# Two buffers instead of three for the low half of a split weight, and a twelfth buffer for raw weights

## The chip, the cores and the metric

The kernel runs on one core of one Trainium2 chip. The metric is the device time of one launch in microseconds (us). Before the change the median of three runs was 1666.89 us (1665.35 to 1670.17).

## The reference

A two-layer encoder trunk over 256 tokens of width 1024, all in float32. Every layer is a mixer, a memory cross-attention and a feed-forward part, each added to the residual stream:

```
for l in range(2):
    xn = rmsnorm(x, norm_mix[l])
    x = x + (even_mixer if l == 0 else odd_mixer)(xn, ...)
    x = x + memory_cross_attention(rmsnorm(x, norm_mem_q[l]), rmsnorm(mem, norm_mem_kv[l]), w_q, w_kv, w_o)
    h = rmsnorm(x, norm_ffn[l])
    x = x + (swiglu(h, gate, up, down)           # width 2816, layer 0
             if l == 0 else moe_swiglu(h, ...))  # top 2 of 8 experts of width 3584, layer 1
return rmsnorm(x, norm_final)
```

The even mixer is a gated MLP over blocks of 128 tokens beside a forgetting attention, whose logits get the cumulated log of a forget gate as a bias. The odd mixer is a differential attention with a relative bias beside a short gated convolution. The weights are read once: 95 MB before the experts and 336 MB in the eight experts.

## The kernel before

**Pieces.** All weights come in pieces of 1 MB (128 partitions x 2048 floats). `load_w` (L108) does three things with each. SyncE's queue (SP) issues the DMA into a raw buffer (L106). ScalarE (ACT) copies the raw piece into `wh`, rounded to the engine format fp32r, in two instructions of 128x1024 (L121). VectorE (DVE) writes the rest, raw minus `wh`, into `wl` (L123), in two instructions of 128x1024 before the experts and in one of 128x2048 in them. TensorE (PE) then multiplies three times: `wh` by the high and by the low half of the activations (L138 and L141, alternating), and after these `wl` by the high half (L144). In three of the eight experts, the small ones (places 2, 4 and 7, at most 64 tokens each), two products are made (L996), again the one with `wl` last. So `wl` is read in the last third or half of a piece's work on PE.

**Buffers.** `wh` and `wl` come from one pool (`wsplit`, L63) with three buffers each. The subtraction for piece j can start when the raw piece has landed, its `wh` is written, and PE has read the `wl` of piece j-3 for the last time. The raw buffers are two before the experts (`rawp`). For the experts the room of tiles that are not needed any more is taken as well, and a pool `raw2` of `RAW2` = 3 buffers is opened: eleven in all, used in turn. The DMA into a raw buffer waits until the subtraction of the piece that had it before has ended.

**Order.** The program is written in one order and a scheduler gives each engine a fixed list at build time, by its own model of what becomes ready when. An engine works through its list in order: an instruction that waits holds up all that stand behind it. In `issue_after` regions (`behind`) the kernel ties an instruction to another by hand. So the place of a split instruction among the norm, softmax and routing steps of its engine depends on when the scheduler believed that a buffer would be free.

**Names.** `cb` (L491, L492) is the bias of the forgetting attention: `cvec` (the cumulated gates) is written to DRAM and read back on all partitions by a DMA from GpSimd's queue (L473), and DVE then adds the mask in two steps. `qT` and `kT` (L478, L481) are that attention's queries and keys, projected from four pieces (0 to 3); `elg` are its logits, `mh`/`ml` and `nh`/`nl` the split memory tokens and the split normalised activations, `tps` transposes on PE, `xs` (L163, L282) and `ms` (L149) steps of a norm. `gcr`/`gcp` (L213, L215) fetch and transpose the gain of the router's norm. `ge` (L906) is the exponential in the router's gates, `sg` (L1032) the SiLU of an expert's gate product, `sgs` (L1028) the copy that stands at that place in a small expert.

**Experts.** An expert has 42 pieces in four chunks of its width: gate, the down projection of the chunk before, up. 128 (or 64) gathered tokens stand still and the weights move. The end (`finish`, L1179 on) scatters the last expert's output and norms the result. The gain of the final norm lies in the buffer that the rotation gives at that point.

Of the kernel before, what the change touches and what calls it, by code (L numbers as in the profile page):

```python
# [12 lines left out]
F32R = mybir.dt.float32r  # L13
# [7 lines left out]
P = 128  # L21
# [6 lines left out]
DFF = 2816  # L28
DFFE = 3584
NE = 8  # L30
RAW2 = 3
WSPLIT = ((0, 0, 4), (1, 0, 4), (0, 4, 8), (1, 4, 8))
WSPLIT_MOE = ((0, 0, 4), (0, 4, 8), (1, 0, 8))
CHUNKS = ((0, 1024), (1024, 1024), (2048, 1024), (3072, 512))
# [21 lines left out]
def trunk_kernel(ctx: ExitStack, tc: tile.TileContext, io, out, stop=None):  # L56
# [37 lines left out]
    def pick(kind):  # L94
        lst = pools[kind]
        p = lst[cnt[kind] % len(lst)]
        cnt[kind] += 1
        return p

    def load_raw(src, a, b, parts=1):  # L100
        p, tag = pick("raw")
        r = p.tile([P, a, b], F32, tag=tag, name="raw")
        m = a // parts
        for i in range(parts):
            with behind(*gate):
                chain["dma"] = nc.sync.dma_start(r[:, i * m:(i + 1) * m, :], src[:, i * m:(i + 1) * m, :])  # L106
            gate.clear()
        return r  # L108

    def load_w(src, a, b, parts=1):  # L110
        r = load_raw(src, a, b, parts)
        p = pick("w")
        wh = p.tile([P, a, b], F32R, tag="wh", name="wh")
        wl = p.tile([P, a, b], F32R, tag="wl", name="wl")
        rf, hf, lf = (v.rearrange("p a b -> p (a b)") for v in (r, wh, wl))
        n = a * b // parts
        for part in range(parts):
            for i, c0, c1 in pools["split"]:
                sl = slice(part * n + c0 * n // 8, part * n + c1 * n // 8)
                if i == 0:  # L120
                    chain["wh"] = nc.scalar.activation(hf[:, sl], rf[:, sl], AF.Copy)  # L121
                elif i == 1:
                    chain["wl"] = nc.vector.tensor_sub(lf[:, sl], rf[:, sl], hf[:, sl].bitcast(F32))  # L123
                else:
                    nc.gpsimd.tensor_sub(lf[:, sl], rf[:, sl], hf[:, sl].bitcast(F32))
        return wh, wl

    def split_to(hi, lo, src):
        return (nc.scalar.activation(hi, src, AF.Copy),  # L129
                nc.vector.tensor_sub(lo, src, hi.bitcast(F32)))  # L130
# [107 lines left out]
    pA = ctx.enter_context(tc.tile_pool(name="acts", bufs=1))  # L238
    ps2 = ctx.enter_context(tc.tile_pool(name="xs", bufs=2))
    with ExitStack() as pre:  # L240
# [48 lines left out]
        def proj_ws(act, w, ncols, c0, into=None):  # L289

            ah, al = act
            wh, wl = load_w(w[:, c0:c0 + 256].rearrange("(k p) n -> p k n", p=P), KT, 256)
            ps = mmp.tile([P, 2, S], F32, tag="mm", name="pws") if into is None else into
            for f in range(2):
                o = ps[:, f, :]
                mm3([(o, wh[:, k, f * P:(f + 1) * P], wl[:, k, f * P:(f + 1) * P], ah[:, k, :], al[:, k, :])
                     for k in range(KT)], True, True, True)
            return ps
# [476 lines left out]
    with ExitStack() as moe:  # L775
        mA = moe.enter_context(tc.tile_pool(name="macts", bufs=1))
        sm = moe.enter_context(tc.tile_pool(name="msmall", bufs=2))
        m2 = moe.enter_context(tc.tile_pool(name="macts2", bufs=2))
        raw2 = moe.enter_context(tc.tile_pool(name="raw2", bufs=RAW2))

        def mbank(shape, name="mm"):
            return trp.tile(shape, F32, tag="tr", name=name)
# [294 lines left out]
        def split_y(yacc, n, pool=mA, tag="y"):  # L1077
            y = pool.tile([P, 2, 512], F32R, tag=tag, name="y")
            split_to(y[:, 0, :], y[:, 1, :], yacc[n])
            return y  # L1080

        def scatter(e, st, y, n):
            sl = slice(n * 512, (n + 1) * 512)
            for t in range(2):
                ps = mbank([P, 512], "sc")
                for i in range(2):
                    nc.tensor.matmul(ps, st[:, t, :], y[:, i, :], start=i == 0, stop=i == 1)
                nc.vector.scalar_tensor_tensor(x[t][:, sl], ps, comb[:, t, e:e + 1], x[t][:, sl],  # L1088
                                               op0=OP.mult, op1=OP.add)
# [4 lines left out]
        if done(4):  # L1094
            return
        pools["raw"] = ([(rawp, "raw")] + [(pA, tag) for tag in ("mh", "ml", "nh", "nl", "K")]
                        + [(raw2, "raw")] * RAW2 + [(pA, "V"), (rawp, "raw")])
        cnt["raw"] = cnt["w"] = 0
# [34 lines left out]
        for e in range(NE):  # L1133
            for c in range(nch):
# [32 lines left out]
                if prev is not None:  # L1167
                    pe, pc, phT, nacc = prev
# [7 lines left out]
                if c == 0:  # L1176
                    yacc = [mmp.tile([P, 512], F32, tag="mm", name=f"y{n}") for n in range(2)]
# [24 lines left out]
        pe, pc, hT, yacc = prev  # L1202
# [3 lines left out]
            down(pc, hT, yacc, i, w2[i])  # L1206

        def last_scatter(n):
            scatter(pe, st, split_y(yacc, n, pA, ("gain", "nh")[n]), n)
        finish(gf, last_scatter)  # L1210


        cv = nc.values_load(cint[0:1, NE:NE + 1], min_val=0, max_val=S + CAP - SCAP,
                            skip_runtime_bounds_check_because="a count of 256 tokens lies in 0..256")
        with tc.If(cv > CAP):
            for e in range(NE):
                for r0 in range(SCAP if e in SMALL else CAP, S, P):
# [26 lines left out]
                    st = m2.tile([P, 2, P], F32, tag="st", name="st_o", bufs=1)  # L1244
# [66 lines left out]
```

## Time and profile before

| | |
|---|---|
| median of three runs | 1666.89 us |
| the profiled execution | 1662.44 us |
| its span in the trace | 1660.7 us |
| PE busy | 1565.1 us (94%) |
| DVE busy | 1263.7 us (76%) |
| ACT busy | 1074.4 us (65%) |
| granted TensorE clock, mean | 0.993 |

The span is what the trace covers, from the first to the last instruction; 1.7 us of the execution lie around it. The busy share is a mean over stages. Until about 640 us (mixers, attentions, dense feed-forward) PE is nearly always busy and DVE is idle for more than a third of the time; in the experts, from about 640 to 1645 us, DVE is busy for 81 to 91% of each stretch, and the DMA engines for 74 to 99%. A row of the timeline gives the start, the duration (of all, where several are taken together: x2, x4), the engine, the line, the operation and its tiles, and in brackets how long the engine stood idle before it and what ended the wait.

### The profile page before, as it was taken

What the parts mean: (1) busy time and instruction counts of PE and PEld (TensorE: products, weight loads), DVE (VectorE), ACT (ScalarE), POOL (GpSimd) and SP (SyncE); (2) the same over time, 40 slices, a digit from 0 to 9 for tenths busy, and PEclk for the clock granted to TensorE, in tenths of its full rate; (3) what the DMA queues carried; (4) which work ended last, traced back from release to release, by engine and by line L of the source; (5) the groups of instructions that cost most, each with busy time, mean ns of one, the idle gap of its engine ahead of it and who ended that gap; (6) DMA issues with size and microseconds to landing.
All of it is one profiled execution on the core that took longest, in us unless ns stands there. A gap on an engine that the chain in (4) does not pass through costs nothing. (4 is left out here: it accounts for less than half of the span.)

```text
span 1660.7 us, 22384 instructions
## 1 busy us (share of the span) xinstructions
PE 1565.1 (94%) x8432; PEld 1305.1 (79%) x8432; DVE 1263.7 (76%) x1216; ACT 1074.4 (65%) x1396; POOL 46.9 (3%) x75
## 2 busy tenths in 40 slices
PE   8999999999999999999999889999888999999885
PEld 7889889999989887888887667777667777777653
DVE  5785665445576657899988888978988978888875
ACT  5555553444554446787777787677777766777775
POOL 1010010000000102000000000000000000000000
PEclk9999999999999999999999999999999999999998
DMA  7556465565535586999999999999999999999980
GB/s 248 166 185 207 145 224 195 180 201 178 190 128 178 185 333 245 345 346 348 359 361 364 350 351 349 339 334 386 341 356 349 333 346 344 339 338 347 356 304 28
DMA packets 175585, 465.03 MB, mean 280 GB/s; under 512 B 9118, under 2 KB 64438, under 8 KB 175340
## 3 DMA queue, kind: packets, MB, share of 16 engines
q1 hardware_dynamic: 174412, 459.80, 77.2%
q0 software_dynamic: 1056, 3.72, 0.7%
q8 instruction: 68, 1.11, 0.3%
q14 instruction: 49, 0.40, 0.1%
HBM read 462.42 MB, written 2.11 MB: 280 GB/s over the span
## 5 line engine op out<-in xcount | busy, mean ns | idle before, releaser
L123 DVE TENSOR_TENSOR wl<-raw,wh 128x2048 fp32r<-128x2048 f32 (+1 forms) x527 | 983.5, 1894 | 232.5 <-ACT wh L121 229.2
L121 ACT ACTIVATE wh<-raw 128x1024 fp32r<-128x1024 f32 x866 | 852.6, 1049 | 280.3 <-PE pws L141 95.1
L138 PE MATMUL gu<-wh,ch 128*128 128x512 f32 x560 | 220.6, 394 | 2.8 <-ACT sg L1032 2.8
L141 PE MATMUL gu<-wh,cl 128*128 128x512 f32 x560 | 219.2, 392 | 0.1
L144 PE MATMUL gu<-wl,ch 128*128 128x512 f32 x560 | 152.8, 395 | 10.5 <-DVE wl L123 10.5
L138 PE MATMUL pws<-nh,wh 128*128 128x256 f32 x560 | 137.2, 283 | 0.0
L141 PE MATMUL pws<-nl,wh 128*128 128x256 f32 x560 | 137.2, 283 | 0.0
L144 PEld LDWEIGHTS gu<-wl,ch 128*128 128x128 f32 x560 | 103.5, 188 | 40.3 <-DVE wl L123 19.1
L138 PEld LDWEIGHTS gu<-wh,ch 128*128 128x128 f32 x560 | 105.1, 188 | 27.1 <-ACT sg L1032 2.9
L996 PE MATMUL gu<-wl,ch 128*128 128x512 f32 x336 | 99.2, 417 | 25.3 <-DVE wl L123 24.3
L141 PEld LDWEIGHTS gu<-wh,cl 128*128 128x128 f32 x560 | 105.2, 188 | 21.9 <-DVE cl L1113 0.5
L141 PE MATMUL y<-wh,hs 128*128 128x512 f32 x280 | 110.9, 396 | 0.0
L138 PE MATMUL y<-wh,hs 128*128 128x512 f32 x280 | 110.4, 394 | 0.0
L138 PEld LDWEIGHTS pws<-nh,wh 128*128 128x128 f32 x560 | 105.9, 189 | 1.3 <-ACT wh L121 0.9
L141 PEld LDWEIGHTS pws<-nl,wh 128*128 128x128 f32 x560 | 105.9, 189 | 0.4
L996 PEld LDWEIGHTS gu<-wl,ch 128*128 128x128 f32 x336 | 58.3, 189 | 56.4 <-DVE wl L123 47.5
L996 PE MATMUL gu<-wh,ch 128*128 128x512 f32 x336 | 96.7, 402 | 4.4 <-ACT wh L121 4.0
L138 PE MATMUL acc<-wh,ch 128*128 128x512 f32 x216 | 84.7, 392 | 0.0
L141 PE MATMUL acc<-wh,cl 128*128 128x512 f32 x216 | 84.4, 391 | 0.0
L996 PEld LDWEIGHTS gu<-wh,ch 128*128 128x128 f32 x336 | 62.7, 190 | 23.6 <-ACT wh L121 10.7
L144 PE MATMUL y<-wl,hs 128*128 128x512 f32 x280 | 79.1, 404 | 2.0 <-DVE wl L123 2.0
L144 PE MATMUL pws<-nh,wl 128*128 128x256 f32 x560 | 78.8, 283 | 0.0
(363 smaller groups left out, 2177.7 us busy)
## 6 DMA issues: line engine op xcount, KB each, us to landing
raw<-in_moe_w_up_dram SPq DMA_DIRECT2D x112, 1024.0 KB, 7.1
raw<-in_moe_w_gate_dram SPq DMA_DIRECT2D x112, 1024.0 KB, 6.7
raw<-in_moe_w_down_dram SPq DMA_DIRECT2D x110, 1024.0 KB, 6.6
raw<-in_mem_w_kv_dram SPq DMA_DIRECT2D x16, 1024.0 KB, 5.2
raw<-in_odd_w_in_dram SPq DMA_DIRECT2D x12, 1024.0 KB, 5.2
raw<-in_ffn_w_gate_dram SPq DMA_DIRECT2D x11, 1024.0 KB, 5.1
raw<-in_ffn_w_up_dram SPq DMA_DIRECT2D x11, 1024.0 KB, 5.1
raw<-in_ffn_w_down_dram SPq DMA_DIRECT2D x11, 1024.0 KB, 4.8
```

Source lines behind the costliest of these rows:

```text
L121: chain["wh"] = nc.scalar.activation(hf[:, sl], rf[:, sl], AF.Copy)
L123: chain["wl"] = nc.vector.tensor_sub(lf[:, sl], rf[:, sl], hf[:, sl].bitcast(F32))
L138: mm = nc.tensor.matmul(ps, ah, bh, start=f, stop=False, skip_group_check=bank)
L141: nc.tensor.matmul(ps, *((ah, bl) if w_left else (al, bh)), start=False, stop=False, skip_group_check=bank)
L144: mm = nc.tensor.matmul(ps, *((al, bh) if w_left else (ah, bl)), start=False, stop=e, skip_group_check=bank)
L996: mm = nc.tensor.matmul(ps, a, b[which], start=f, stop=e)
```

## The change

`wl` gets a buffer count of its own, two, so that the subtraction for piece j waits until PE has read the `wl` of piece j-2 (before: j-3). `wh` keeps three. The room, 8 KB in each partition, goes to a fourth buffer of `raw2`: the rotation in the experts has twelve raw buffers instead of eleven. With twelve, the buffers that the gain of the final norm and the last piece come to lie in are others, and the second half of the last scatter takes the room of `mh` instead of `nh`.

```
-RAW2 = 3
+RAW2 = 4
...
         wh = p.tile([P, a, b], F32R, tag="wh", name="wh")
-        wl = p.tile([P, a, b], F32R, tag="wl", name="wl")
+        wl = p.tile([P, a, b], F32R, tag="wl", name="wl", bufs=2)
...
-            scatter(pe, st, split_y(yacc, n, pA, ("gain", "nh")[n]), n)
+            scatter(pe, st, split_y(yacc, n, pA, ("gain", "mh")[n]), n)
```

The scheduler gives other lists to DVE, ACT, PE and SP from the start to the beginning of the third expert. GpSimd's list, and from there on those of the four engines, are the same as before.

The first place is DVE's list in the forgetting attention, where the bias `cb` is made. Each L123 of 128x1024 is half a piece. Before:

```order
L468 TENSOR_SCALAR fncs<-fcs 4x256
L123 TENSOR_TENSOR wl<-raw,wh 128x1024 x4
L491 TENSOR_TENSOR cb<-cb,cmask 128x4x128
L492 TENSOR_TENSOR cb<-cb,cmask 128x4x128
L123 TENSOR_TENSOR wl<-raw,wh 128x1024
L149 TENSOR_SCALAR ms<-ss 128x1
L282 SCALAR_TENSOR_TENSOR xs<-xs,rs,gain 128x1024
```

And now:

```order
L468 TENSOR_SCALAR fncs<-fcs 4x256
L123 TENSOR_TENSOR wl<-raw,wh 128x1024 x2
L491 TENSOR_TENSOR cb<-cb,cmask 128x4x128
L123 TENSOR_TENSOR wl<-raw,wh 128x1024 x2
L492 TENSOR_TENSOR cb<-cb,cmask 128x4x128
L123 TENSOR_TENSOR wl<-raw,wh 128x1024
L149 TENSOR_SCALAR ms<-ss 128x1
```

The four halves ahead of `cb` are pieces 2 and 3. Piece 3, the second one of the keys, now stands behind the first step of `cb`.

The second place is ACT's list in the first expert, third chunk: the router's two `ge` and the two `sg` among the copies of the weights (numbers in the names tell the pieces apart). Before:

```order
L121 ACTIVATE wh_6749<-raw_6747 128x1024
L906 ACT_TABLE_LOAD
L906 ACTIVATE ge_6512<-ge_6512,comb_5835 128x1
L121 ACTIVATE wh_6749<-raw_6747 128x1024
L121 ACTIVATE wh_6768<-raw_6766 128x1024
L906 ACTIVATE ge_6532<-ge_6532,comb_5835 128x1
...
L121 ACTIVATE wh_6817<-raw_6815 128x1024 x2
L1032 ACT_TABLE_LOAD
L1032 ACTIVATE sg_6822<-gu_6640,rs_6272 128x512
L1032 ACTIVATE sg_6822<-gu_6641,rs_6272 128x512
```

And now:

```order
L906 ACT_TABLE_LOAD
L906 ACTIVATE ge_6512<-ge_6512,comb_5835 128x1
...
L1032 ACT_TABLE_LOAD
L1032 ACTIVATE sg_6822<-gu_6640,rs_6272 128x512
L906 ACT_TABLE_LOAD
L906 ACTIVATE ge_6532<-ge_6532,comb_5835 128x1
...
L1032 ACT_TABLE_LOAD
L1032 ACTIVATE sg_6822<-gu_6641,rs_6272 128x512
```

The first `sg` has moved in between the two `ge`, and with it ACT loads its function table four times where it loaded it twice.

The third place is ACT's list where the third expert, the first of the small ones, begins. Before:

```order
L121 ACTIVATE wh_8118<-raw_8116 128x1024 x2
L121 ACTIVATE wh_8135<-raw_8133 128x1024 x2
L1028 ACTIVATE sgs_8207<-gu_8069,rs_7941 128x512
L1028 ACTIVATE sgs_8207<-gu_8070,rs_7941 128x512
L121 ACTIVATE wh_8150<-raw_8148 128x1024 x2
```

And now:

```order
L121 ACTIVATE wh_8118<-raw_8116 128x1024 x2
L121 ACTIVATE wh_8135<-raw_8133 128x1024 x2
L121 ACTIVATE wh_8150<-raw_8148 128x1024 x2
L1028 ACTIVATE sgs_8207<-gu_8069,rs_7941 128x512
L1028 ACTIVATE sgs_8207<-gu_8070,rs_7941 128x512
```

The copy of one piece (`wh_8150`) has moved ahead of the two `sgs`.

## Rows read from the trace of the kernel before

**Rows 1.** The page: engines' busy time, DMA share in 40 slices, issue to landing
```profile
PE 1565.1 (94%) x8432; PEld 1305.1 (79%) x8432; DVE 1263.7 (76%) x1216; ACT 1074.4 (65%) x1396; POOL 46.9 (3%) x75
...
raw<-in_moe_w_up_dram SPq DMA_DIRECT2D x112, 1024.0 KB, 7.1
```
**Rows 2.** Windows: us, busy PE, PEld, DVE, ACT, POOL; clock, DMA share, GB/s
```profile
640.00:760.00 120.00, 117.15 (x549) 97.01 (x548) 109.36 (x125) 96.11 (x110) 1.95 (x2) 1.00 0.91 339
760.00:883.00 123.00, 123.00 (x555) 100.96 (x555) 110.64 (x68) 94.84 (x104) 0.00 (x0) 1.00 0.99 365
```
**Rows 3.** Waits, SP's queue, 640 to 1645 us: total us, times, longest
```profile
SPq L106 <- DVE wl L123: 618.8, 264, 6.7
```
**Rows 4.** Waits of DVE for landing pieces, 600 to 1645 us (all)
```profile
DVE wl L123 <- DMA raw<-in_moe_w_up_dram: 2.2, 3, 1.0
DVE wl L123 <- DMA raw<-in_moe_w_gate_dram: 0.8, 2, 0.5
```
**Rows 5.** Timeline, DVE: one piece of the dense feed-forward, one of the second expert
```profile
304.30 2.36 DVE L123 TENSOR_TENSOR wl<-raw,wh 128x1024 fp32r<-128x1024 f32 x2 [3.34 <-ACT wh L121]
...
808.62 2.29 DVE L123 TENSOR_TENSOR wl<-raw,wh 128x2048 fp32r<-128x2048 f32 x1 [0.47 <-ACT wh L121]
```
**Rows 6.** Timeline, PE: products with `wl`, two pieces earlier and same piece
```profile
308.72 1.12 PE L144 MATMUL pwu<-nh,wl 128*128 128x256 f32 x8
...
317.08 1.12 PE L144 MATMUL pws<-nh,wl 128*128 128x256 f32 x8
...
809.05 1.08 PE L144 MATMUL gu<-wl,ch 128*128 128x512 f32 x4
...
814.64 1.09 PE L144 MATMUL y<-wl,hs 128*128 128x512 f32 x4
```
**Rows 7.** Timeline, DVE, around `cb`
```profile
26.90 2.36 DVE L123 TENSOR_TENSOR wl<-raw,wh 128x1024 fp32r<-128x1024 f32 x2 [0.55 <-ACT wh L121]
36.72 0.69 DVE L491 TENSOR_TENSOR cb<-cb,cmask 128x512 f32<-128x512 f32 x1 [7.46 <-DMA cb<-cvec]
37.33 0.69 DVE L492 TENSOR_TENSOR cb<-cb,cmask 128x512 f32<-128x512 f32 x1
```
**Rows 8.** Timeline, PE, around piece 3 and the logits
```profile
35.82 1.11 PE L144 MATMUL pws<-nh,wl 128*128 128x256 f32 x8
...
41.26 1.09 PE L265 MATMUL tps<-ident,xs 128*128 128x128 f32 x8 [1.26 <-DVE ms L149]
...
46.21 1.22 PE L499 MATMUL elg<-kT,qT 128*128 128x256 f32 x2 [0.55 <-DVE ml L130]
```
**Rows 9.** Timeline, ACT and SP: copies of pieces 4 and 5, issues
```profile
36.70 2.94 ACT L121 ACTIVATE wh<-raw 128x1024 fp32r<-128x1024 f32 x3
...
26.38 3.28 SPq L106 DMA_DIRECT2D raw<-in_even_w_in_dram  x2
```
**Rows 10.** Timeline, PE: waits in the odd layer
```profile
423.82 0.63 PE L265 MATMUL tps<-ident,xs 128*128 128x128 f32 x4 [0.70 <-DVE xs L163]
...
485.79 0.30 PE L714 MATMUL ont<-ident,on 128*128 128x128 f32 x1 [0.87 <-DVE on L710]
...
550.60 0.19 PE L215 MATMUL gcp<-ident,gcr 8*128 8x8 f32 x1 [2.48 <-DMA gcr<-in_norm_ffn_dram]
```
**Rows 11.** Timeline, ACT: table loads in the first expert
```profile
706.46 1.28 ACT L906 ACT_TABLE_LOAD   x1
707.76 0.29 ACT L906 ACTIVATE ge<-ge,comb 128x1 f32<-128x1 f32 x1
...
718.96 1.28 ACT L1032 ACT_TABLE_LOAD   x1
```
**Rows 12.** Timeline, DVE and PE: the piece that follows the table loads
```profile
718.92 2.28 DVE L123 TENSOR_TENSOR wl<-raw,wh 128x2048 fp32r<-128x2048 f32 x1
...
721.84 1.09 PE L144 MATMUL y<-wl,hs 128*128 128x512 f32 x4
```
**Rows 13.** Timeline, DVE: entry of the third expert
```profile
890.42 8.89 DVE L123 TENSOR_TENSOR wl<-raw,wh 128x2048 fp32r<-128x2048 f32 x4 [2.06 <-ACT wh L121]
```

## Prediction
> **What bounds the kernel now.** I read the page first: PE is busy for 1565.1 us of a span of 1660.7 us, at nearly the full granted clock [rows 1]. What PE does isn't changed, so the time can move only by PE's idle stretches, some 96 us in all. Then the windows: in the first expert PE is busy for 117.15 of 120 us and in the second for all of 123, while DVE has 109.36 and 110.64 us of work [rows 2]. So in these two experts, and in everything before them, PE is the bound, and DVE runs ahead of it. Third, the waits. SP's queue waits 618.8 us, 264 times, for a subtraction to release a raw buffer [rows 3]: the engines that eat the weights pace the DMA, not the other way round. In all the experts DVE waits 3.0 us, five times, for a piece to land [rows 4], and ACT and PE never. Last the timeline at the places where the new lists differ from the old.
>
> **The twelfth raw buffer: 0.** A piece lands some 7.1 us after its issue [rows 1]. A deeper queue can at most remove the 3.0 us of [rows 4]; it doesn't move the pace. Bounds 0 and -3.0; I take 0, since only the release changes, and that comes from the same subtractions.
>
> **The missing third `wl` buffer where nothing is moved: 0.** In the dense feed-forward, DVE subtracts a piece at 304.30 [rows 5], and PE first uses it at 317.08; the piece two earlier is read until 308.72 + 1.12 = 309.84 [rows 6]. With two buffers the subtraction starts there, 5.5 us later, and ends at 309.84 + 2.36 = 312.2: 4.9 us early still. In the second expert the subtraction at 808.62 [rows 5] would wait for 809.05 + 1.08 = 810.13, end at 812.42, and be needed at 814.64 [rows 6]: a lead of 3.7 us shrinks to 2.2. The other pieces of both stages repeat this with a lead that stays above 1.7 us. What is queued behind a waiting subtraction on DVE (a split of activations, an `sg`) comes up to 1.5 us later and has about that much to spare. Price 0, if the cover is gone up to 1.5 us per place.
>
> From the third expert on the lists are the same, and DVE isn't three pieces ahead of PE any more: the third buffer lies unused, and the rest of the run is moved as a whole.
>
> **What the new lists cost.** Four places carry the sum.
>
> *The bias `cb`: +3.5 us.* Its first step waits on a DMA and starts at 36.72, after 7.46 us of idleness. Piece 3 was subtracted before that, from 26.90 to 29.26 [rows 7], and PE wanted it at 35.82 [rows 8]. Now it stands behind that step: it can run from 37.33 and takes 2.36 us, to 39.69. Of PE's eight products the first four could run once the first half is there, at 38.5; the other four, due at 35.82 + 0.48 = 36.30, wait for 39.69: PE is 3.4 us late. Part of it falls into idle time that PE has right behind: 1.26 us at 41.26 for the memory norm and 0.55 us at 46.21 for the logits [rows 8]. The norm on DVE, though, stands behind `cb`'s second step, which ends at 39.69 + 0.6 instead of 38.0, so these waits move along by 2.3 us. That is the lower end. The upper end comes from SP: the raw buffer of piece 3 goes to piece 5, whose DMA was the second of two that SP had issued by 29.66 [rows 9], right after the subtraction. Now it is issued at 39.7. It lands between 42.6 (1 MB at the 365 GB/s of [rows 2]) and 46.8 (the 7.1 us of [rows 1]). ACT has piece 5's two copies (the last two of the three at 36.70 [rows 9], 2.0 us) ahead of the second `kT` and the memory's `mh` (0.6 us each), and DVE's `ml` needs 0.6 more. With the early landing this is done before the norm's transposes; with the late one the first `ml` is there at 50.6, and the logits, before at 46.21, come 4.5 us late. Value 3.5, about the middle of 2.3 to 4.5.
>
> *Norms and softmaxes before the experts: +3.1 us.* Halves of a subtraction that wait for PE now stand ahead of steps that PE waits for. In the norm before the odd mixer a half (1.2 us) comes between the residual and `xs`; PE's wait of 0.70 us there [rows 10] grows by up to as much: +0.7. In the differential attention two halves move in between the softmax steps (+1.2) and a piece of 2.36 us moves out from ahead of the norm for which PE waits 0.87 us [rows 10]: +0.5. At the router's gain PE arrives four products of 0.235 us earlier at a transpose that waits for a DMA of its own, 2.48 us now [rows 10]: +0.9. A few like these (the first softmax, the memory attentions, the routing) are worth 0 to 2 together, and I take 1.0. Sum 3.1, range 0 to 4.1: a wait that PE meets late anyway, after the 3.5 us, can swallow a part.
>
> *The table loads: +1.0 us.* The first expert's third chunk has two more of them, 1.28 us each [rows 11]: 2.56 us more on ACT, and one `sg` of 0.65 us earlier in the list, all ahead of the copy that releases the subtraction at 718.92. That copy was done 1.9 us before it. So the subtraction starts 1.3 us later and ends at 722.5; PE wants it at 721.84 [rows 12], 0.65 us late, and the second `sg` with its table load makes it about 1.0 in the next piece but one. Range 0 to 2.6, the whole of the ACT time.
> The Trainium skill ("ScalarE: Activation LUTs", What ACT_TABLE_LOAD costs) gives a switch 1283 ns for the load and some 1380 ns for a drain, 2.66 us together. Here the load ends at 707.74 and the next activation starts at 707.76 [rows 11]: the load agrees, the drain doesn't show. By the page the two loads would be 5.3 us, and this term some 2.7 us larger, near 3.7; I go by the row.
>
> *The third expert's entry: -1.2 us.* DVE waits 2.06 us for a copy at 890.42 [rows 13]; ACT now has it ahead of two `sgs` of 1.27 us together. DVE sets the pace there, so about that much is gained, less a little for `sgs`. Range -2.1 to 0.
>
> **The sum.** 3.5 + 3.1 + 1.0 - 1.2 = +6.4 us. The profiled execution took 1662.44 us (span 1660.7), so it would take 1668.8. It lies 4.45 us below the median of the runs shown, which is within their spread; the same +6.4 on the median gives 1673.3 us.
>
> **Rivals.**
> *No change.* The 3.4 us at piece 3 are swallowed by later waits for DMAs that come at a fixed time, and the small terms are lost in PE's idle time. Before the third expert PE idles some 18 us in all, so there is room. Against it: the largest of these waits are themselves behind the chain that is delayed. +0 to +3, about 1668.
>
> *Faster.* It has its place at the entry of the third expert: the copy moved ahead there gives all 2.06 us [rows 13], the twelfth buffer removes the 3.0 us of waits for landing pieces [rows 4], and `cb` costs only what doesn't fit into the 1.81 us of PE's idle time right behind it, 1.6. Together -3.5 us, with the 3.1 of the norms hidden: 1663.4. It decides when the bias lands: if `cvec` comes 3 us earlier, piece 3 costs nothing, and it is -5. Against it: nothing in the change makes that DMA earlier.
>
> *A bubble in each piece.* The Trainium skill ("Perfetto Trace Analysis", Identifying Performance Opportunities) says that the same gap again and again on the busiest engine can mean too few buffers for the next tile. As a mechanism here: each of the 83 pieces from the fourth of the first expert to the end of the second starts its subtraction only when PE has finished the piece two before, DVE loses up to 1.5 us of its lead each time, and its spare time (12.4 of 123 us in the second expert, 10.6 of 120 in the first [rows 2]) is used up. If a fifth of the 83 come 0.5 us late, that is 8 us more: 1681.7. Against it: the loss of a lead is paid once and not per piece, as PE's use and DVE's start are then tied at a distance of two pieces.
>
> That the change doesn't do what it says isn't likely: the lists differ, and the buffer counts are fixed at build time.
>
> **How the numbers follow.** About 0.3% (5 us) is what a measurement of this kernel tells from no change. Forecast (+2 to +12) 0.62, no change (0 to +3) 0.22, bubbles (+12 to +18) 0.07, faster (-5 to 0) 0.09. Of the forecast's case two thirds lie above +5, the rest counts as the same: slower 0.42 + 0.07 + 0.04 for runs that a small shift in the medians takes over the bound = 0.53; faster 0.07, since of the faster case only a part passes the bound, and the base of three runs is itself uncertain; same 0.40. The range takes in the terms' bounds: their lower ends give 2.3 + 0 + 0 - 2.1 - 3.0 = -2.8, their upper ends 4.5 + 4.1 + 2.6 + 0 = +11.2, and 2 us of spread of the runs on the upper side: 1664 to 1680.5.
>
> **What would show it.** Right: in the new trace PE waits 3 us for `wl` at about 36 to 40 us; the logits start at 49 to 51; the wait before `gcp` is near 3.4; ACT has four table loads between 705 and 730; DVE's 2.06 us at the third expert are gone; and from there to the end both traces run at one distance, 6.4 us. Wrong: if PE has new waits for `wl` all through the first two experts, it is the bubbles; if the distance is under 2 us at 640 us, the order cost nothing; if it changes between the third expert and the end, the claim that the rest is only moved fails.

## The result, and the profile after

The changed kernel takes 1678.2 us (median of five runs, 1674.0 to 1679.84), the kernel before on the same chip 1665.68 us (1665.32 to 1670.17). The ratio is 1.0065, with a 95% interval of 1.0051 to 1.0079: 10.8 us slower (0.0065 x 1666). The profiled execution took 1674.0 us, its span is 1672.1 us.

The page of the kernel after; it answers to the first line of [rows 1]:

```profile
PE 1570.2 (94%) x8432; PEld 1305.6 (78%) x8432; DVE 1263.7 (76%) x1216; ACT 1080.4 (65%) x1398; POOL 47.8 (3%) x75
```

ACT has two instructions and 6 us more, GpSimd 0.9 us more; PE has the same 8432 products and 5.1 us more for them; its mean granted clock is 0.991, and was 0.993. PE's idle time in the span grew from 95.6 to 101.9 us.

The waits of SP's queue, 640 us to the end, as [rows 3]:

```profile
SPq L106 <- DVE wl L123: 649.1, 272, 8.1
```

The subtractions still pace the DMA. DVE's waits for landing pieces, 3.0 us in [rows 4], have no row any more.

The windows of the kernel after, first expert, with the columns of [rows 2]:

```profile
640.00:760.00 120.00, 113.65 (x517) 92.94 (x516) 101.15 (x117) 91.65 (x104) 7.09 (x4) 0.97 0.86 317
```

GpSimd works 7.09 us in this stretch, where it had 1.95: its piece came later. The granted clock was 1.00 and is 0.97.

The best view is a difference of two traces: take the time at which each piece's last product ends on PE, subtract the time of the same product in the trace of before, and see by how much this distance grows in each stretch (us; the stretches go by the times of before, and those left out move by 0.2 or less in every column). Names of the columns are those of the experiments below; *again* is the same kernel profiled once more.

| stretch of before, us | what lies there | after | again | x_pre3 | x_pool | x_gates | x_cb | x_all |
|---|---|---|---|---|---|---|---|---|
| 0 to 34 | first pieces | -0.6 | -0.5 | -0.6 | +1.8 | +0.3 | -0.2 | +0.1 |
| 34 to 72 | `cb` | -0.1 | +0.1 | +0.9 | +1.3 | +2.5 | +0.2 | -2.6 |
| 72 to 423 | layer 0 | +2.3 | +2.7 | -0.2 | +3.1 | +2.4 | +2.0 | +2.4 |
| 423 to 538 | odd norm, differential attention | +1.5 | +1.5 | +0.2 | +1.5 | +1.5 | +1.5 | +1.5 |
| 538 to 556 | router's gain | +0.8 | +0.5 | -1.6 | +0.9 | +1.0 | +0.7 | +0.8 |
| 556 to 640 | layer 1 to the experts | 0.0 | +0.1 | +2.6 | 0.0 | +1.6 | +1.1 | -0.1 |
| 640 to 651 | first pieces of the experts | **+4.0** | **+4.0** | **+4.0** | 0.0 | +4.0 | +4.0 | 0.0 |
| 657 to 672 | first SiLU | +1.4 | +2.7 | +0.5 | +1.5 | +2.8 | +2.8 | +1.5 |
| 712 to 762 | table loads | +1.8 | +1.8 | +1.8 | +1.8 | +0.4 | +1.8 | +0.4 |
| 877 to 902 | entry of the third expert | -0.7 | -0.7 | -0.7 | +1.0 | -0.7 | -0.7 | +1.0 |
| 902 to 1569 | the rest | -0.3 | +0.1 | +0.5 | +0.5 | +0.2 | +0.1 | -0.3 |
| 1569 to the end | | +1.5 | +0.3 | +0.8 | 0.0 | +1.0 | +0.3 | +1.5 |
| all | | 11.7 | 12.6 | 8.4 | 13.4 | 17.0 | 13.7 | 6.4 |

The profiled execution of before was a short one (1662.44 us), so these totals lie above what the ratios say. A term that is the same to 0.1 us in several columns belongs to the kernel; of one that changes from profile to profile (the first and the last row, `cb`, the first SiLU) a single column says little.

The largest term stands in no sentence of the prediction. GpSimd's timeline at the start of the experts, before and then after:

```profile
635.42 6.53 POOL L125 TENSOR_TENSOR wl<-raw,wh 128x512 fp32r<-128x512 f32 x4 [0.87 <-ACT wh L121]
```

```profile
644.27 7.09 POOL L125 TENSOR_TENSOR wl<-raw,wh 128x512 fp32r<-128x512 f32 x4 [5.86 <-issue]
```

GpSimd subtracts the experts' third piece (L125, in four quarters). Before, it did so as soon as `wh` was there; now it waits for PE's first piece and starts 8.85 us later, of which 3.9 are the distance that everything had by then. DVE and PE of the kernel after in the same place:

```profile
638.62 2.29 DVE L123 TENSOR_TENSOR wl<-raw,wh 128x2048 fp32r<-128x2048 f32 x1
...
646.95 3.29 DVE L123 TENSOR_TENSOR wl<-raw,wh 128x2048 fp32r<-128x2048 f32 x1 [4.24 <-issue]
```

```profile
651.41 0.50 PE L144 MATMUL gu<-wl,ch 128*128 128x512 f32 x1 [2.06 <-POOL wl L125]
```

And the tile `wl` there, count and shortest/median/longest in ns, then first and last start:

```profile
L125 POOL TENSOR_TENSOR wl<-raw,wh x4: 1300/1308/3329, 644.3 to 648.0; 128x512 fp32r<-128x512 f32 x4
L123 DVE TENSOR_TENSOR wl<-raw,wh x2: 2286/2788/3290, 638.6 to 646.9; 128x2048 fp32r<-128x2048 f32 x2
```

DVE starts the next piece at 646.95, while GpSimd is at its third quarter: DVE's subtraction takes 3.29 us instead of 2.29, GpSimd's last quarter 3.33 instead of 1.30, and PE stands idle for 2.06 us. The other 2 us are clock: in 650 to 660 us the granted clock was 0.83 (row with x_apart below).

The two engines met before the change too. GpSimd's quarters in the trace of before:

```profile
L125 POOL TENSOR_TENSOR wl<-raw,wh x4: 1287/1288/2767, 635.4 to 640.7; 128x512 fp32r<-128x512 f32 x4
```

The first quarter took 2.77 us, beside DVE's subtraction of 634.75 to 637.03. PE didn't need the piece yet, and no wait of PE came of it.

### The profile page after: what moved, and what is told of

Same layout as the page of the kernel before. It is cut to its first block, busy times and chain, and to the rows that moved or that the text cites. A ratio compares the mean times of both kernels' runs of the same rounds, so it can differ in the third digit from the quotient of the medians.

```text
span 1672.1 us, 22491 instructions
## 1 busy us (share of the span) xinstructions
PE 1570.2 (94%) x8432; PEld 1305.6 (78%) x8432; DVE 1263.7 (76%) x1216; ACT 1080.4 (65%) x1398; POOL 47.8 (3%) x75
## 5 line engine op out<-in xcount | busy, mean ns | idle before, releaser
L123 DVE TENSOR_TENSOR wl<-raw,wh 128x2048 fp32r<-128x2048 f32 (+1 forms) x527 | 986.1, 1897 | 230.6 <-ACT wh L121 85.0
L144 PE MATMUL gu<-wl,ch 128*128 128x512 f32 x560 | 154.5, 397 | 12.6 <-DVE wl L123 10.5
```

Of the source, the lines that this page charges most:

```text
L144: mm = nc.tensor.matmul(ps, *((al, bh) if w_left else (ah, bl)), start=False, stop=e, skip_group_check=bank)
```

## The experiments

One run is the changed kernel once more; all others are edits of it or of the kernel before that alter order or buffers, and all compute the whole reference. Ratios are to the kernel before, run beside each.

**x_wl2: two `wl`, eleven raw buffers.** The half of the change without the twelfth raw buffer; the lines are those in which it differs from the changed kernel.

```
-RAW2 = 4
+RAW2 = 3
...
-            scatter(pe, st, split_y(yacc, n, pA, ("gain", "mh")[n]), n)
+            scatter(pe, st, split_y(yacc, n, pA, ("gain", "nh")[n]), n)
```

> One part alone: two wl buffers, eleven raw buffers. Theory 1 (the whole loss comes from the lists and waits that the missing wl buffer makes): the lists are those of the changed kernel up to the last expert, so 1676 to 1680 us, ratio to before near 1.0065, and the distance to the trace of before follows that of the changed kernel piece by piece. Rival (the twelfth raw buffer, and the places it gives to the gain of the final norm, cost something): back by a few us, 1668 to 1674, with the distance different in the last expert.

Measured: 1681.21 us, ratio 1.0096 (1.0075 to 1.0117). All of the losses are there (+4.0 and +1.8 among them), and the entry of the third expert costs +0.97 where the changed kernel has -0.69: the lists are those of after but for this place, where `wh_8150` stands behind the `sgs` again, and the end. DVE at the entry:

```profile
907.60 6.70 DVE L123 TENSOR_TENSOR wl<-raw,wh 128x2048 fp32r<-128x2048 f32 x3 [1.89 <-ACT wh L121]
```

So the losses are owed to `wl`, and the gain at the entry to the twelfth raw buffer; whether through the list or through the buffer itself, x_wl2sgs asks.

**x_pool: GpSimd's piece gets a raw buffer for its `wl`,** so that it need not wait for PE.

```
-        wl = p.tile([P, a, b], F32R, tag="wl", name="wl", bufs=2)
+        wl = spare.tile([P, a, b], F32R, tag="raw", name="wl") if spare else p.tile([P, a, b], F32R, tag="wl", name="wl", bufs=2)
...
-            w_first.append(gate_piece(wg, 0, 0, 2))
+            w_first.append(gate_piece(wg, 0, 0, 2, raw2))
```

> The changed kernel, but the wl of the experts' third piece, the one that GpSimd subtracts, gets a room of its own (one of the raw2 buffers), so it need not wait for PE to read the first piece. Theory 1 (GpSimd's 7 us start 9 us later because of that wait, PE idles 2.1 us and its clock falls for some us after it): GpSimd's start goes back from 644 to about 639, PE's idle 2.06 us at 651 are gone, the distance at the experts' fourth piece is 3.9 and not 7.9 us, and if the second stretch of low clock (670 to 680 us) follows from the first, another 1.3 us are gone: 1672 to 1674 us. Rival (what is lost there is the lists' order on DVE, where pieces wait for PE): the distance still grows to 7 to 8 us by the fourth piece and the time stays at 1677 to 1680.

Measured: 1675.26 us, 1.0054 (1.0035 to 1.0074). GpSimd:

```profile
643.88 6.56 POOL L125 TENSOR_TENSOR wl<-raw,wh 128x512 fp32r<-128x512 f32 x4 [0.83 <-ACT wh L121]
```

It starts 8.46 us later than in before, which is just the distance of this run at that point (8.5), and the first pieces of the experts cost 0.05 instead of 4.0. The ratio isn't clearly below that of the changed kernel (1.0065, and 1.0051 when it ran again): ACT's list at the third expert falls back to that of before and takes 1.7 us of the 4.0 back (+1.0 there instead of -0.7). The 1672 to 1674 us that were expected were missed. GpSimd and DVE overlap here as well:

```profile
L125 POOL TENSOR_TENSOR wl<-raw,wh x4: 1279/1292/2806, 643.9 to 649.1; 128x512 fp32r<-128x512 f32 x4
```

One quarter takes 2.81 us, and PE doesn't wait: an overlap that comes early enough costs nothing.

**x_gates: the first `sg` of the third chunk stays behind the second `ge`,** as before.

```
-                nc.scalar.activation(ge[:, 1:2], ge[:, 0:1], AF.Exp, scale=comb[:, t, NE:NE + 1])
+                chain["ge"] = nc.scalar.activation(ge[:, 1:2], ge[:, 0:1], AF.Exp, scale=comb[:, t, NE:NE + 1])
...
-                sg = gated(e, gu, rs)
+                with behind(*(("ge",) if (e, c) == (0, 2) else ())): sg = gated(e, gu, rs)
```

> The changed kernel, with the first expert's third sg tied behind the second ge of the router, so that ACT loads its table twice there and not four times. Theory 1 (the two more loads of 1.28 us cost the 1.8 us by which the distance grows at 727 to 740 us): PE's wait of 1.32 us at 733 is gone, the distance stays at 9.2 us there, time 1675 to 1677. Rival (two wl buffers cost it, since DVE's lead is thin there anyway): the distance grows to 11 as before, time unchanged.

Measured: 1677.42 us, 1.0070 (1.0047 to 1.0093): no gain that the ratio could show, but the term falls from 1.8 to 0.4. The first expert's third chunk in the kernel after, ACT and then PE, and PE in x_gates:

```profile
716.67 1.28 ACT L906 ACT_TABLE_LOAD   x1
...
720.44 1.28 ACT L1032 ACT_TABLE_LOAD   x1
...
722.44 1.28 ACT L906 ACT_TABLE_LOAD   x1
...
731.64 1.28 ACT L1032 ACT_TABLE_LOAD   x1
```

```profile
732.78 1.20 PE L144 MATMUL y<-wl,hs 128*128 128x512 f32 x4 [1.32 <-DVE wl L123]
```

```profile
738.21 1.20 PE L144 MATMUL y<-wl,hs 128*128 128x512 f32 x4 [0.26 <-DVE wl L123]
```

With two loads instead of four PE's wait for that `wl` shrinks from 1.32 to 0.26 us.

**x_cb: both steps of `cb` stay behind piece 3,** as before.

```
-            nc.vector.tensor_tensor(cb[:, :, S:384], ...
+            with behind("wl"): nc.vector.tensor_tensor(cb[:, :, S:384], ...
-            nc.vector.tensor_tensor(cb[:, :, P:S], ...
+            with behind("wl"): nc.vector.tensor_tensor(cb[:, :, P:S], ...
```

> The changed kernel, with both steps of the bias cb tied behind piece 3's subtraction, as before the change; all other lists stay. Theory 1 (the move cost nothing on balance: with the next raw piece issued later, the DMA of cb has the engines for itself and lands 2.4 us earlier, and PE's clock does not fall at 43 to 49 us): cb lands at 36 to 37 us again, the idle stretches of before (1.3, 0.9, 0.6 us) are back, the granted clock falls again at 40 to 50 us, and the distance at piece 6 is within 1 us of the changed kernel's -0.7. Rival (the forecast: the move costs 2.3 us at least, and something else hid it): the distance at piece 6 falls to -3 or below, time 1674 to 1676.

Measured: 1674.22 us, 1.0049 (1.0032 to 1.0067). The stretch of `cb` reads +0.2, no better than after's -0.1. That isn't the order but the clock. Windows of 45 to 50 us, before, x_cb, after and x_all (the third number from the end is the granted clock):

```profile
45.00:50.00 5.00, 4.46 (x13) 3.22 (x12) 4.59 (x9) 0.62 (x2) 0.00 (x0) 0.54 0.85 255
```

```profile
45.00:50.00 5.00, 4.57 (x11) 3.67 (x12) 4.18 (x7) 0.41 (x1) 0.00 (x0) 0.54 0.67 230
```

```profile
45.00:50.00 5.00, 3.32 (x17) 2.85 (x18) 4.43 (x9) 2.36 (x5) 0.00 (x0) 1.00 0.82 250
```

```profile
45.00:50.00 5.00, 5.00 (x24) 4.24 (x25) 4.17 (x8) 0.00 (x0) 0.00 (x0) 1.00 0.76 220
```

Before and x_cb ran here at 0.54, after and x_all at 1.00. x_cb and x_all have the same order of `cb` and differ by 2.8 us in this stretch (+0.2, -2.6), while PE is idle in it for 2.4 and 2.6 us: that is the clock. After against x_all, both at 1.00, the order is worth -0.12 - (-2.58) = 2.46 us.

That is one pair, and another says the opposite. y_sgs3 (below) has before's order here, and a granted clock of 1.00 from 35 to 60 us, yet its stretch reads +0.4. Its bias landed late:

```profile
39.65 0.69 DVE L491 TENSOR_TENSOR cb<-cb,cmask 128x512 f32<-128x512 f32 x1 [7.75 <-DMA cb<-cvec]
45.00:50.00 5.00, 2.46 (x16) 1.81 (x15) 5.00 (x7) 2.04 (x4) 0.00 (x0) 1.00 0.55 149
```

Over all profiles, the seven with piece 3 ahead of `cb` (before, x_cb, x_all, x_pre3, y_sgs3, y_poolwait, y_poolwait2) lie between -2.6 and +1.5 in this stretch, 0.3 on the mean; the seven with the new order (after, again, x_pool, x_gates, x_wl2, x_wl2sgs, x_apart) between -0.1 and +3.4, 1.7 on the mean. So the order costs some 1.4 us, with a spread within each group of over 3 us: that it costs something is likely, how much is not shown.

**after_again: the changed kernel once more,** unchanged.

> The changed kernel once more, unchanged, as the measure for the other runs of this call. Theory 1: 1674 to 1680 us; in the trace +4 us between the experts' first and fourth piece, +1.8 at pieces 26 to 30, -0.7 at 80 to 90 come again to 0.1 us, while what is lost before the experts and at piece 8 changes by 1 to 3 us from run to run with the granted clock. Rival (the terms are chance of one profile): they differ as much as the rest.

Measured: 1674.85 us, 1.0051 (1.0034 to 1.0068). Its column above shows which terms repeat.

**x_all: x_pool, x_gates and x_cb in one.**

> The changed kernel with the three undoings together: piece 3 subtracted ahead of cb, a room of its own for the piece that GpSimd subtracts, one table load pair less. Theory 1 (the terms add): against before 0.2 us at cb, 4 to 5 us for the other moved halves before the experts, 1.4 to 2.9 at piece 8, 0.4 at the table loads, 1.0 at the third expert: 7 to 9 us in the trace, so some 4 to 5 us less than the changed kernel (which has cb 1.5, GpSimd 4.0, tables 1.8, entry -0.7): 1670 to 1673 us. Rival (the places hide one another, so that another stall appears when one goes): 1674 to 1678.

Measured: 1670.84 us, 1.0021 (1.0008 to 1.0034): 3.5 us over before. The changed kernel beside it (after_again) was 8.5 us over before, so about 5 us come back, as the terms added up would have it. What is left in its profile are the 4.7 us of 72 to 556 us and the entry's +1.0; the -2.6 at `cb` is in part clock, and so is the +1.5 in each of two other stretches.

**x_pre3: three `wl` buffers before the experts, two in them,** and twelve raw buffers.

```
+        ...; pools["wl3"] = pre.enter_context(tc.tile_pool(name="wl3", bufs=1))
...
-        wl = p.tile([P, a, b], F32R, tag="wl", name="wl", bufs=2)
+        wl = pools["wl3"].tile(...) if "wl3" in pools and cnt["w"] % 3 == 0 else p.tile([P, a, b], F32R, tag="wl", name="wl", bufs=2)
```

> Three wl buffers before the experts, two in them, twelve raw buffers: the lists are those of the kernel before up to the routing, and two-buffer lists in the experts. Theory (the loss has two halves, the moved halves before the experts and the overlap with the table loads in them): between pieces 6 and 84 the distance to before changes by less than 1 us (the changed kernel: 4.5 to 5 us), at cb by less than 1 us at the same clock; in the experts the 4.0 us of the overlap and the stretch of low clock at piece 8 come again. Time some 5 us below the changed kernel, 1669 to 1673. Rival (the moved halves cost little by themselves, and the 4.6 us between pieces 6 and 84 come from the clock): the distance still grows there by 3 us or more.

Measured: 1671.31 us, 1.0022 (1.0013 to 1.0031). With the third buffer back the lists up to the routing are those of before, and the terms of 72 to 538 us are gone; +4.0, +1.8 and -0.7 stay. (This puts back both, the buffer that is waited for and the order; it doesn't tell the two apart.) (Its -1.6 and +2.6 right after stand in y_poolwait too, as -1.65 and +2.23, and that one has all the lists of before: they belong to the execution, not to an order.) PE's waits of the kernel after in the odd layer, those that answer to [rows 10], and the first two of x_pre3 that do:

```profile
427.86 0.63 PE L265 MATMUL tps<-ident,xs 128*128 128x128 f32 x4 [0.50 <-DVE xs L163]
...
487.87 0.30 PE L714 MATMUL ont<-ident,on 128*128 128x128 f32 x1 [1.17 <-DVE on L710]
...
490.46 0.30 PE L714 MATMUL ont<-ident,on 128*128 128x128 f32 x1 [0.77 <-DVE on L710]
...
553.54 0.20 PE L215 MATMUL gcp<-ident,gcr 8*128 8x8 f32 x1 [3.05 <-DMA gcr<-in_norm_ffn_dram]
```

```profile
486.12 0.30 PE L714 MATMUL ont<-ident,on 128*128 128x128 f32 x1 [0.85 <-DVE on L710]
...
550.92 0.20 PE L215 MATMUL gcp<-ident,gcr 8*128 8x8 f32 x1 [2.42 <-DMA gcr<-in_norm_ffn_dram]
```

The wait for `on` grew from 0.87 to 1.17 and got a second one of 0.77 beside it, the wait at the gain from 2.48 to 3.05; the odd norm's fell from 0.70 to 0.50.

**y_poolwait, y_poolwait2: is it GpSimd's wait, or what it runs into?** x_pool takes the late start away. Two theories: waiting alone costs the 4 us, or it costs them because GpSimd's late piece runs at the same time as DVE's next one. x_pool has shown that such an overlap alone costs nothing. These two are the kernel before, with one more `wl` taken ahead of GpSimd's piece, so that it must wait with three buffers too. In the first the extra tile is never written, in the second GpSimd writes one column of it before and one after its piece.

```
+            d = wp.tile([P, 2, 1024], F32R, tag="wl", name="wl")[:, 0, 0:1].bitcast(F32); nc.gpsimd.memset(d, 0.0)
             w_first.append(gate_piece(wg, 0, 0, 2))
+        with behind("pl"): nc.gpsimd.memset(d, 0.0)
```

> The kernel before with the one wait added: an unused wl tile is taken from the pool ahead of the experts' third piece, so GpSimd's wl goes to the buffer of the first piece and waits for PE to have read it; from the fourth piece on there are three buffers again, and every engine's list stays. Theory 1 (the wait of GpSimd costs 4 us by itself, with or without the rest of the change): GpSimd starts 8 to 9 us later than in the kernel before, PE idles 2 us for its wl, the distance to before grows by 3.9 to 4.0 us between the experts' first and fourth piece, time 4 us (up to 5.5 with a second stretch of low clock at piece 8) above before: 1669 to 1672 us. Rival (it costs that only together with the two-buffer lists): under 1 us, time as before.

> The kernel before with the one wait added, now with the extra wl tile held (a memset of one column ahead of and one behind GpSimd's subtraction), since an unused tile had given its room back. GpSimd's wl of the experts' third piece has to go where the first piece's was; after it there are three buffers again. Theory 1 (that wait costs 4 us by itself): GpSimd starts 8 to 9 us later than in the kernel before, PE idles 2 us for its wl, the distance grows by 3.9 to 4.0 us between the experts' first and fourth piece, time 4 to 5.5 us above before. Rival (it costs that only together with the two-buffer lists): under 1 us between these pieces.

Measured: y_poolwait 1668.01 us, 1.0000 (0.9986 to 1.0015), but GpSimd started at 635.54 as before: the unwritten tile's room was given back, no wait came about, and it tells nothing of the theories. y_poolwait2 1666.5 us, 1.0000 (0.9988 to 1.0012), and there GpSimd did wait:

```profile
642.66 5.06 POOL L125 TENSOR_TENSOR wl<-raw,wh 128x512 fp32r<-128x512 f32 x4 [8.12 <-issue]
```

The first pieces of the experts cost 0.65 us, not 4. The wait alone is not the price. In this kernel DVE's next subtraction waited for GpSimd's last write, so the two didn't run together.

**x_apart: the changed kernel, with GpSimd's late piece kept apart from DVE's next one.** GpSimd writes a column of that piece's `wl` first, so DVE can start only when GpSimd is done. GpSimd still waits for PE.

```
-        for part in range(parts):
+        for part in ([nc.gpsimd.memset(lf[:, 0:1].bitcast(F32), 0.0)][:0] if e0.pop("hold", 0) else []) + list(range(parts)):
...
-            w_first.append(gate_piece(wg, 0, 0, 2))
+            w_first.append(gate_piece(wg, 0, 0, 2)); e0["hold"] = 1
```

> The changed kernel, but DVE's subtraction of the experts' fourth piece waits until GpSimd has ended that of the third (GpSimd then writes one column of the fourth piece's wl first, which DVE overwrites). All lists stay. Theory 2, after the wait alone had cost 0.65 us: in the changed kernel both engines are released by PE within 3 us of each other, so their subtractions overlap; GpSimd's longest quarter takes 3.3 us instead of 1.3 and DVE's 3.3 instead of 2.3, and it is this that leaves PE idle for 2 us and lets its clock fall. Then apart GpSimd needs 5.1 us from 644 or so, PE waits 0.6 us for it and at most 0.6 for DVE, and the distance between the first and the fourth piece grows by 0.7 to 1.3 us instead of 4.0: 1671 to 1675 us. Rival (theory 1, the late start of GpSimd with two-buffer lists is enough): 3.5 to 4.5 us as before, or more, since DVE is held up too.

Measured: 1675.95 us, 1.0048 (1.0032 to 1.0065). The stretch costs 0.67 us instead of 4.0. The tile `wl` there, and DVE's timeline:

```profile
L125 POOL TENSOR_TENSOR wl<-raw,wh x4: 1288/1294/1297, 649.2 to 652.9; 128x512 fp32r<-128x512 f32 x4
```

```profile
654.30 8.90 DVE L123 TENSOR_TENSOR wl<-raw,wh 128x2048 fp32r<-128x2048 f32 x4 [6.61 <-POOL wl L117]
```

Every quarter takes 1.29 us again, though DVE now waits 6.61 us and starts later. The time of the runs does not show the 3.3 us: 1.0048 is no clear gain on 1.0065 and 1.0051, it lies 1 us above the 1671 to 1675 that were expected, and this profile has +2.7 us at `cb` and +2.9 at the first SiLU. Windows of 650 to 660 us, of the kernel after and of x_apart:

```profile
650.00:660.00 10.00, 8.59 (x31) 6.90 (x32) 5.72 (x4) 5.87 (x6) 1.36 (x1) 0.83 0.76 290
```

```profile
650.00:660.00 10.00, 9.96 (x43) 7.57 (x42) 5.70 (x3) 6.47 (x8) 4.26 (x5) 1.00 0.46 165
```

PE is kept busy, and the granted clock is 1.00 where it was 0.83. So late without overlap costs 0.65 to 0.67 us (y_poolwait2, x_apart), overlap without lateness 0.05 (x_pool), and both together 4.0: PE's idle 2.06 us and the low clock behind it.

**x_wl2sgs: x_wl2 with `wh_8150` ahead of the `sgs`.** Is the entry's gain the list's, or the twelfth buffer's itself?

```
+ ...; chain[f"g{i}"] = chain["wh"]
...
+                with behind(*(("g1",) if (e, c) == (2, 0) else ())): sg = gated(e, gu, rs)
```

> Two wl buffers, eleven raw buffers, and ACT's list at the third expert's entry as the changed kernel has it with twelve. Theory 1 (the twelfth raw buffer acts by that list alone): at pieces 80 to 90 the distance to before falls by 0.7 us, as in the changed kernel, instead of rising by 1.0, and the time is that of the changed kernel run beside it within 2 us. Rival (the twelfth buffer gains by itself): the distance still rises there, or the time stays 3 us above the changed kernel's.

Measured: 1679.38 us, 1.0070 (1.0053 to 1.0088). The entry costs -0.08: of the 1.67 us between x_wl2 and after the list alone gives 1.05. The rest is probably that DVE, ahead now, meets pieces that haven't landed:

```profile
918.49 2.29 DVE L123 TENSOR_TENSOR wl<-raw,wh 128x2048 fp32r<-128x2048 f32 x1 [2.08 <-DMA raw<-in_moe_w_up_dram]
```

Its waits for landing pieces, 600 us to the end, are 9.6 us here (2.3 in x_wl2), and none in after and in after_again.

**y_sgs3: the kernel before, with that order at all three small experts.**

```
-                    wh, wl = ready.pop(0) if ready else gate_piece(w, e, c, i)
+                    wh, wl = ready.pop(0) if ready else gate_piece(w, e, c, i); chain[f"g{i}"] = chain["wh"]
...
-                sg = gated(e, gu, rs)
+                with behind(*(("g1",) if e in SMALL and c == 0 else ())): sg = gated(e, gu, rs)
```

> The kernel before (three wl, eleven raw buffers), with the one move of the changed kernel that gained: in the first chunk of the three small experts ACT copies one weight piece ahead of the sgs. Theory 1 (that move is what the twelfth raw buffer was worth, through the scheduler's model and not through the DMA): at the third expert's entry the trace gains 1.2 to 1.7 us on before; at the other two small experts' entries, where DVE does not wait that long, 0 to 1.5 each. 1661 to 1664 us. Rival (the gain came from the DMA running one piece further ahead): no gain at any of the three, 1665.

Measured: 1663.8 us, 0.9977 (0.9966 to 0.9989). It beats both kernels. The three entries give -1.23, -0.94 and -0.97 us; the wait of 2.06 us in [rows 13] is gone:

```profile
890.28 13.30 DVE L123 TENSOR_TENSOR wl<-raw,wh 128x2048 fp32r<-128x2048 f32 x6
```

## Why the prediction was right, and where not

The time was forecast at 1673.3 us and slower; it came out slower, 4.9 us above that. The time alone would flatter the steps: of the four named terms two came out within 0.8 us, one was outside its range, the size of one is not settled, and the largest loss was in none of them.

**Right.** No bubble in each piece: the distance moves by less than 0.1 us between 672 and 712 us, by 0.2 between 762 and 877, and between the third expert and 1569 us by 0.3. Two buffers cost nothing in these stretches, as said; GpSimd's one piece is the exception. The rest of the run is only shifted. The router's gain: forecast 0.9, measured 0.8; the wait reads 3.05 where 3.4 was announced. The sign of three of the four named places; that of `cb` is likely but not settled. (Three slips of counting change nothing: from the fourth piece of the first expert to the end of the second there are 81 pieces, not 83; 8 us more than 1673.3 are 1681.3, not 1681.7; and the upper end of the range adds up to 1680.1, not 1680.5.)

**`cb`, forecast +3.5: mis-sized, some 1.4 on the mean of seven profiles against seven, and -0.1 in the two first ones.** The mechanism came as told: piece 3 behind `cb`'s first step, PE waiting twice for it, the logits late. DVE and PE of the kernel after, answering to [rows 7] and [rows 8]:

```profile
34.25 0.69 DVE L491 TENSOR_TENSOR cb<-cb,cmask 128x512 f32<-128x512 f32 x1 [8.48 <-DMA cb<-cvec]
34.86 2.36 DVE L123 TENSOR_TENSOR wl<-raw,wh 128x1024 fp32r<-128x1024 f32 x2
```

```profile
36.13 0.74 PE L144 MATMUL pws<-nh,wl 128*128 128x256 f32 x4 [0.73 <-DVE wl L123]
37.27 0.73 PE L144 MATMUL pws<-nh,wl 128*128 128x256 f32 x4 [0.40 <-DVE wl L123]
...
46.68 0.70 PE L499 MATMUL elg<-kT,qT 128*128 128x256 f32 x2 [2.28 <-DVE ml L130]
```

The bias landed earlier (34.25 against 36.72), so PE waited 0.73 and 0.40 us for piece 3, and not 3.4; the logits' wait grew from 0.55 to 2.28, and they started at 46.68, not at 49 to 51. The step that failed is the bias's landing time, which the forecast took over from before's trace. Against its rival *faster* it held that nothing makes this DMA earlier; it came earlier in all seven profiles with the new order (last section). That the first two profiles show no loss is due also to before's profile, which had 0.54 of the clock right there.

**Norms and softmaxes, forecast +3.1: 4.6 (2.3 + 1.5 + 0.8), above its 0 to 4.1.** x_pre3 shows that most of it, 72 to 538 us, goes with the missing buffer and the lists that it makes. At the gain, profiles of equal clock (0.91) take 18.2 us in before and y_sgs3 and 18.7 to 19.2 in those with the new lists. By parts the step failed more than by its sum: the odd norm, +0.7 forecast, cost nothing (0.70 became 0.50); the differential attention cost 1.4 and not 0.5; and the "few like these" of layer 0, 1.0, cost 2.3, about half at 72 to 113 us and 0.7 at 173 to 204. Single halves there were not put back one by one.

**Table loads, forecast +1.0: 1.8, within its 0 to 2.6.** x_gates takes 1.35 of it away. Each load is 1.28 us and the next activation starts 0.02 us later (722.44 to 723.74), as in [rows 11].

**Entry, forecast -1.2: -0.7.** x_wl2 adds what I hadn't seen: this gain hangs on the twelfth raw buffer, which I had set at 0. Set against the same `wl` with eleven raws it is worth 1.67 us there: 1.05 by the list, and 0.6 that are left, probably by landing pieces.

**Missed: GpSimd, +4.0.** The order of GpSimd's list was unchanged, and I took an unchanged list for unchanged work. The step that failed is "where nothing is moved: 0": I held DVE's subtractions against PE's reading and never asked the same of the one that GpSimd makes, 8.85 us later now. x_pool takes the 4.0 away, y_poolwait2 shows that the wait by itself isn't the price, and x_apart that the overlap with DVE, once the piece is late, is.

The Trainium skill has the rule that fits ("SBUF — State Buffer", Who interferes with whom): a DVE instruction with two SBUF inputs and a GpSimd instruction that reads SBUF contend, since they share a read interface, and the sharing is an exclusive lock in which the order of issue decides who blocks. The trace agrees: DVE's 3.29 us are its 2.29 and the 1.0 that GpSimd's third quarter still had from 646.95 to 648.0; the last quarter's 3.33 are its 1.30 and 2.0 of the time that DVE then took, until 650.24.

**The clock, +1.4 and +1.5 in the profile.** These are not shown to be the change's; see the last section. The forecast had no term for it.

**Together.** The terms that repeat give 4.0 + 4.6 + 1.8 - 0.7 = 9.7 us, and with 1.4 for `cb` 11.1, an estimate, beside the 10.8 of the ratio. The forecast's 6.4 had the right sign with 4.0 missing, 1.5 and 0.8 too little at the norms and the tables, 0.5 too much gain at the entry, and some 2 too much at `cb`.

## What to carry to other kernels

A buffer count that a build-time scheduler sees acts in two ways: what waits longer (4.0 us at one piece of GpSimd, whose list is unchanged, and nothing that shows in the steady stretches), and what the scheduler puts elsewhere because it believes it waits (1.8 us of table loads; the 4.6 us before the experts belong to both ways together). Look at every engine that writes the buffer, also the one whose list is unchanged: a piece that starts later can meet another engine's work just when its reader wants it. And a gain that a change brings by a new order (-0.7 at one entry) can be had without the change, by asking for that order (-3.1 at three).

## What the runs showed of the hardware

**The granted clock after the first SiLU.** PE stands idle for the first `sg` of the experts, whatever the kernel: 2.85 us before, 2.89 after.

```profile
662.48 0.50 PE L138 MATMUL gu<-wh,ch 128*128 128x512 f32 x1 [2.85 <-ACT sg L1032]
```

```profile
670.40 0.79 PE L138 MATMUL gu<-wh,ch 128*128 128x512 f32 x1 [2.89 <-ACT sg L1032]
```

The first product takes 0.50 us in the one and 0.79 in the other. The windows around it of before, y_poolwait (the same lists, and GpSimd at the same time) and after:

```profile
660.00:670.00 10.00, 7.52 (x37) 6.26 (x38) 7.38 (x8) 7.76 (x10) 0.00 (x0) 1.00 0.83 333
```

```profile
660.00:670.00 10.00, 7.15 (x28) 5.91 (x27) 6.67 (x6) 5.72 (x8) 0.00 (x0) 0.69 0.97 369
```

```profile
670.00:680.00 10.00, 9.60 (x40) 8.07 (x41) 6.60 (x6) 6.15 (x8) 0.00 (x0) 0.84 0.49 176
```

After this idle time before's profile kept the full clock (2.4 GHz) and y_poolwait's fell toward the lower level (1.2 GHz), and lost 2.6 us by it; y_sgs3 lost 1.6 and y_poolwait2 nothing. So the 1.4 to 2.8 us that most kernels with two `wl` show there can't be put down to the change from two profiles. Over all of them the clock fell there in nine of the ten profiles with two `wl` in the experts and in two of the four with three; whether the change makes it fall more often is open. It differs between executions of the same lists also at 45 us and at the end, where after's granted clock was 0.74 from 1620 to 1640 us and after_again's 0.91. Why it falls in one execution and not in the other is open.

**The bias's way through DRAM.** From the start of `fncs` to that of `cb` it took 10.9 to 11.5 us in the seven profiles where piece 5's DMA was issued behind it, and 11.6 to 14.3 us in the seven where it was issued ahead; that it was this DMA which slowed it was not tried by itself.
